# Moving operands on a 1152-byte pitch in a decoder trunk of float32 matmuls

## The chip, the cores and the metric

The kernel runs on one core of a Trainium2 chip. The metric is the device time of one execution in microseconds; a kernel is timed in several runs, and the median counts.

## The reference

A trunk of two layers over 528 tokens (16 learned meta tokens and 512 of the input) of width 1024. Each layer adds half a SwiGLU block, a mixer and half a second SwiGLU block to the residual stream, with an RMS norm ahead of each. The mixer of the first layer is chunked retention with four heads, that of the second is gated linear attention (GLA). All is float32.

```python
def swiglu(x, w_in, w_out):                  # w_in 1024 x 5632, w_out 2816 x 1024
    gate, up = jnp.split(x @ w_in, 2, axis=-1)
    return (jax.nn.silu(gate) * up) @ w_out

for i in range(2):
    h = h + 0.5 * swiglu(rmsnorm(h, norm_ffn1[i]), ffn1_w_in[i], ffn1_w_out[i])
    hn = rmsnorm(h, norm_mix[i])
    mix = retention(hn, ...) if i == 0 else gla(hn, ...)
    h = h + mix
    h = h + 0.5 * swiglu(rmsnorm(h, norm_ffn2[i]), ffn2_w_in[i], ffn2_w_out[i])
h = rmsnorm(h, final_norm)[:, 16:]
```

## The kernel before, in words

The residual stream lies transposed in SBUF: eight tiles x of 128 channels by 528 tokens. The stages follow each other: SwiGLU f10, retention, SwiGLU f20, SwiGLU f11, GLA, SwiGLU f21.

**A product in three.** Every float32 operand is split into a rounded high part and a low part, and a product is three matmuls in a row (mm3, lines 401 to 404): high weights with high tokens (L402), high weights with low tokens (L403), low weights with high tokens (L404). So the moving operands, the tokens, are read in the order high, low, high, then the same for the next block k of 128 input channels. Each matmul covers 264 tokens, half of the 528; in the last SwiGLU, f21, 256 tokens, since the meta tokens are no longer needed.

**Units.** Most projections are done as units: a 2 x 2 block product (two halves of the input channels, two output tiles, two halves of the tokens) in seven products instead of eight, by a Winograd form of Strassen's scheme. Its seven steps (unit_steps, from L589; the order is W.UNIT, L68) each take one weight matrix and one token matrix: a11 reads the first half of the tokens of the first four channel blocks (in uh and ul), a12 and s4 read the last four (both halves), and s1, s2, s3 and a22 read four sums of those, made once for each stage and kept in th (high) and tl (low). Each step is four blocks k and so twelve matmuls. For the output product of SwiGLU the hidden values of a pair of tiles are kept with their sums in tiles H, seven slots of high parts and seven of low ones.

**Where the moving operands lie.** The normed input: tiles uha and ula of 8 x 528 floats, so one block is 2112 bytes after another and the second half of the tokens 1056 after the first (L372 to L374). The sums: th and tl of 4 x 4 x 264 floats, block by block, the four sums of a block 1056 bytes apart (L666). H: 2 x 7 x 264 floats (L727). Retention's gated output og: 4 x 528 floats for each part. uh and ul are used again by every stage.

**Around the products.** Weights come by DMA on SP (raw) and with an accumulating DMA on POOL (pairs), are split by ScalarE (L160) and VectorE (L161) into whi and wlo, and are requested several products ahead. After each step of a unit, ScalarE or VectorE takes the result out of its PSUM bank; a unit has an evacuation tile su (four slots of 264 floats, three buffers, L636), and the values of a pair (gated, L703) and the sums that hidden makes of them (L728) use the same three buffers. u_sums (L573) makes the sums of the normed input of one block and splits all four at once; scaled (L473) writes one block of gained input as high part (ScalarE) and low part (VectorE) when the stage before hands it on; renorm (L694) writes the blocks again once the norm's factor is known. The framework sets the order of the work on each engine by the order of the program and by a head start given to evacuations (urgent, L379); an instruction waits for the tiles that it reads or overwrites.

Of the kernel before, what the change touches and what calls it, by code (L numbers as in the profile page):

```python
# [16 lines left out]
P = 128  # L17
# [35 lines left out]
PW = 512  # L53
AHEAD = 4
# [162 lines left out]

@with_exitstack
def trunk(ctx, tc, a):
# [135 lines left out]
    causal = const.tile([P, P], F32, name="causal")  # L355
    nc.sync.dma_start(causal, a["tri"][1])
    ctail = const.tile([3 * MR, MR], F32, name="ctail")
    for g in range(3):
        S.copy(ctail[g * MR:(g + 1) * MR], causal[g * MR:(g + 1) * MR, g * MR:(g + 1) * MR])
# [7 lines left out]
    half_neg = const.tile([P, 8], F32, name="half_neg")  # L367
    V.memset(half_neg, -0.5)
# [7 lines left out]
    rc = upool.tile([P, 8], F32, tag="rc", name="rc")  # L376

# [60 lines left out]
    def rsqrt_rows(sq, parts, width, name, finish):  # L438
# [13 lines left out]
        G.tensor_tensor(r[:w, :nj], ms[:w, :nj], half_neg[:w, :nj], ALU.pow)  # L452
# [12 lines left out]
    def enter(gcol, by, lag=1, lag2=1):  # L465
# [6 lines left out]

        def scaled(d, parts="hl"):  # L473
            g = gains[:, gcol + d:gcol + d + 1]
            hi, lo, src = uh[d][:, t0:], ul[d][:, t0:], x[d][:, t0:]
            with urgent():
                if "h" in parts:
                    S.activation(hi, src, AF.Copy, scale=g)
                if "l" in parts:
                    V.scalar_tensor_tensor(lo, src, g, hi.bitcast(F32), ALU.mult, ALU.subtract)  # L480
# [37 lines left out]
        def stats():  # L518
# [12 lines left out]
            for (b0, w, nb, m), c in zip(by, cols):  # L531
# [3 lines left out]
                G.tensor_tensor(r, ms[:w, :nb], half_neg[:w, :nb], ALU.pow)  # L535
# [28 lines left out]
    def t_sums(t, b22_b11, b12, b21):  # L564


        if b12 is not None:
            V.tensor_sub(t[:, :2], b22_b11, b12.unsqueeze(1).broadcast_to([P, 2, b12.shape[1]]))
            V.scalar_tensor_tensor(t[:, 2], b22_b11[:, 0], -1.0, t[:, 1], ALU.mult, ALU.subtract)
        if b21 is not None:  # L570
            V.scalar_tensor_tensor(t[:, 3], b21, -1.0, t[:, 2], ALU.mult, ALU.subtract)

    def u_sums(pool, name, halves, normed, hi, lo):  # L573
# [15 lines left out]
    def unit_steps(key, name, order, halves, nk, rhs, places, row1, c22, c21, behind=None):  # L589
# [8 lines left out]
        def step(q):  # L598
# [6 lines left out]
            for k in range(nk):  # L605
                with tc.issue_after(behind.ins) if behind else ExitStack():
                    ends["unit"] = mm3(to[into], *W.at(w, k * P), *rhs(what, k), k == 0 and into not in started,
                                       k == nk - 1, skip_group_check=True)
# [21 lines left out]
    def unit(key, name, order, halves, nk, rhs, pool, row1, c22, c21, behind=None):  # L630
# [8 lines left out]
        for st in unit_steps(key, name, order, halves, nk, rhs, places, row1, c22, c21, behind):  # L639
            st()  # L640

    def quarters(halves, th, tl):

        tl = tl if isinstance(tl, list) else [tl[:, k] for k in range(4)]
        wd = width(halves)

        def rhs(what, k):
# [4 lines left out]
            return th[:, k, i, :wd], tl[k][:, i, :wd]  # L652
# [4 lines left out]
    def ffn(which, layer, halves, gcol, feed, late=False):  # L657
# [5 lines left out]
        with tc.tile_pool(name=f"h_{me}", bufs=4) as hp, tc.tile_pool(name=f"t_{me}", bufs=1) as tp, \  # L663
                tc.tile_pool(name=f"u_{me}", bufs=3) as up_, psum_pool(4) as pp:
            other["pool"] = pp
            th, tl = [tp.tile([P, 4, 4, 264], F32R, tag=f"t{i}", name=f"t{i}{me}") for i in "hl"]  # L666
            rhs_in = quarters(halves, th, tl)
            H, normed = {}, {}
            groups = GROUPS if feed else LAST_GROUPS

            def place(j):


                if j not in normed:
                    t = hp.tile([P, 4 * T + 4 * 264], F32, tag="H", name=f"un{me}{j}")
# [12 lines left out]
            def sums(j):  # L688
                norm(j)
                for i in range(2):  # L690
                    k = 2 * j + i
                    u_sums(up_, f"{me}{k}", halves, normed[j][:, i].rearrange("p h t -> p (h t)"), th[:, k], tl[:, k])

            def renorm():  # L694
                for h, r0, r1 in ((0, a0, a1), (1, a0, a1), (1, b0, b1)):
                    for j in range(2):
                        k = 4 * h + 2 * j
                        split(uha[:, k:k + 2, r0:r1], ula[:, k:k + 2, r0:r1], normed[j][:, :, 1 - h, r0:r1])
# [4 lines left out]
            def gated(f):  # L703
# [4 lines left out]
                return up_.tile([P, 4, 264], F32, tag="su", name=f"y{me}{f}")[:, :, :wd]  # L708

            def hidden(f, y, part=None):  # L710

                gi = [g[0] <= f < g[1] for g in groups].index(True)
                if feed is None and gi == len(groups) - 1:
                    h = hp.tile([P, 2, 2, T], F32R, tag="H", name=f"h{me}{f}")
                    for i in range(2):
                        split(pair(h[:, 0, i, :], halves), pair(h[:, 1, i, :], halves), y[:, 2 - 2 * i:4 - 2 * i])
                elif part == 1:
                    h, t = halfway.pop()
# [1363 lines left out]
```

## Time and profile before

| | |
|---|---|
| median of three runs | 2070.16 us (2069.03 to 2070.55) |
| the profiled execution's own time | 2071.41 us |
| its span | 2069.6 us |
| TensorE busy | 2057.5 us, 16335 matmuls |
| weight loads busy | 2012.9 us |
| VectorE busy | 1790.8 us |
| ScalarE busy | 1200.2 us |
| GpSimd busy | 208.8 us |

A matmul's duration in the profile (about 285 ns for 264 columns) holds its way through the array and overlaps the next ones; how fast they follow each other is read from their start times. A group's line names the line of the kernel, the engine, the operation, output and inputs with buffer numbers left out, the shape and the count, then busy time in us, mean ns of one, and the idle time ahead of it.

### The profile page before, as it was taken

To read this page: it belongs to the slowest core of one execution; us is meant where nothing else is said; L and a number is where in the kernel's file an instruction comes from. 1 tells how busy PE (TensorE), PEld (TensorE's weight loads), DVE (VectorE), ACT (ScalarE), POOL (GpSimd) and SP (SyncE) were. 2 spreads that over 40 slices of the span, in tenths; PEclk is the share of its full clock that TensorE was granted. 3 is DMA by queue.
4 is the path that set the end of the run, shared out by engine and by line. 5 is a ranking of instruction groups with operands and counts; after the bars stand their busy time and mean duration, and the time that the engine had idled before them with its cause. 6 is when DMAs were issued, how large, how long until landed. Compare 5 with 4: busy or idle time off the path is not lost.

```text
span 2069.6 us, 42946 instructions
## 1 busy us (share of the span) xinstructions
PE 2057.5 (99%) x16335; PEld 2012.9 (97%) x16335; DVE 1790.8 (87%) x3218; ACT 1200.2 (58%) x2365; POOL 208.8 (10%) x181
## 2 busy tenths in 40 slices
PE   9999999999999999999999999999999999999998
PEld 9999999999999999999999999999999988999998
DVE  8988889978686889988889998889897968998886
ACT  5756566554545455656666565666645445666664
POOL 1011111010101000111111011111001000111110
PEclk9999999999999999999999999999999999999999
DMA  7676777355555532776776476677614351687772
GB/s 224 154 193 158 193 185 185 107 144 132 146 132 138 136 104 70 184 191 158 195 188 172 111 180 179 162 197 177 194 57 119 91 165 61 161 214 174 183 179 72
DMA packets 176112, 318.84 MB, mean 154 GB/s; under 512 B 17569, under 2 KB 40737, under 8 KB 175905
## 3 DMA queue, kind: packets, MB, share of 16 engines
q1 hardware_dynamic: 133856, 237.04, 34.6%
q0 software_dynamic: 40896, 75.51, 23.5%
q10 hardware_dynamic: 1152, 3.55, 0.5%
q8 instruction: 128, 2.10, 0.4%
q14 instruction: 80, 0.65, 0.1%
HBM read 311.76 MB, written 4.26 MB: 153 GB/s over the span
## 4 chain that ended last, share of the span: by engine, by line
PE 95%; DVE 2%; ACT 1%; issue 1%; DMA 0%; POOL 0%; SPq 0%; POOLq 0%; ACTq 0%; DVEq 0%
PE po_r L403 2%; PE po_r L402 2%; PE po_r L404 2%; PE Xf20o L402 1%; PE Xf10o L402 1%; PE Xf11o L402 1%; PE Xf10o L404 1%; PE Xf10o L403 1%; PE Xf20o L403 1%; PE Xf20o L404 1%; PE Xf11o L403 1%; PE Xf11o L404 1%; PE lv L1614 1%; PE Xf20u L402 1%; PE Xf11u L402 1%; PE Xf21u L404 1%
## 5 line engine op out<-in xcount | busy, mean ns | idle before, releaser
L160 ACT CAST whi<-raw 128x512 fp32r<-128x512 f32 (+1 forms) x893 | 525.6, 606 | 482.3 <-DVE raw L166 92.2
L161 DVE TENSOR_TENSOR wlo<-raw,whi 128x512 fp32r<-128x512 f32 (+1 forms) x893 | 584.1, 669 | 143.8 <-ACT whi L160 134.7
L160 ACT CAST whi<-pair 128x512 fp32r<-128x512 f32 (+1 forms) x304 | 183.5, 604 | 122.2 <-PE Xf11u L403 7.3
L161 DVE TENSOR_TENSOR wlo<-pair,whi 128x512 fp32r<-128x512 f32 (+1 forms) x304 | 202.0, 664 | 6.4 <-ACT whi L160 5.0
L129 POOL DMA_DIRECT2D pair<-in_f_in x73 | 88.5, 1213 | 725.4 <-DVE wlo L161 313.6
L166 DVE TENSOR_TENSOR raw<-pair,raw 128x512 f32<-128x512 f32 (+1 forms) x146 | 97.3, 667 | 2.6
L168 DVE TENSOR_TENSOR raw<-raw,raw 128x512 f32<-128x512 f32 (+1 forms) x146 | 97.3, 666 | 2.5
L129 POOL DMA_DIRECT2D pair<-in_f_out x44 | 53.2, 1208 | 379.1 <-DVE wlo L161 208.8
L402 PE MATMUL po_r<-ogh,whi 128*128 128x264 f32 x256 | 73.0, 285 | 0.0
L403 PE MATMUL po_r<-ogl,whi 128*128 128x264 f32 x256 | 73.0, 285 | 0.0
L404 PE MATMUL po_r<-ogh,wlo 128*128 128x264 f32 x256 | 72.8, 285 | 0.0
L129 POOL DMA_DIRECT2D pair<-in_ret_in x20 | 24.3, 1215 | 301.8 <-DVE wlo L161 90.7
L402 PE MATMUL Xf20o<-hf,whi 128*128 128x264 f32 x176 | 50.8, 289 | 0.2
L402 PE MATMUL Xf11o<-hf,whi 128*128 128x264 f32 x176 | 50.8, 289 | 0.2
L402 PE MATMUL Xf10o<-hf,whi 128*128 128x264 f32 x176 | 50.8, 289 | 0.2
L403 PE MATMUL Xf10o<-hf,whi 128*128 128x264 f32 x176 | 50.0, 284 | 0.0
L403 PE MATMUL Xf11o<-hf,whi 128*128 128x264 f32 x176 | 50.0, 284 | 0.0
L403 PE MATMUL Xf20o<-hf,whi 128*128 128x264 f32 x176 | 50.0, 284 | 0.0
L404 PE MATMUL Xf10o<-hf,wlo 128*128 128x264 f32 x176 | 49.9, 284 | 0.0
L404 PE MATMUL Xf11o<-hf,wlo 128*128 128x264 f32 x176 | 49.9, 284 | 0.0
L404 PE MATMUL Xf20o<-hf,wlo 128*128 128x264 f32 x176 | 49.9, 284 | 0.0
L402 PEld LDWEIGHTS po_r<-ogh,whi 128*128 128x128 f32 x256 | 48.3, 189 | 0.0
(1007 smaller groups left out, 8523.8 us busy)
## 6 DMA issues: line engine op xcount, KB each, us to landing
raw<-in_f_in SPq DMA_DIRECT2D x277, 256.0 KB, 4.5
pair<-in_f_in SPq DMA_DIRECT2D x150, 256.0 KB, 4.7
pair<-in_f_in POOLq DMA_DIRECT2D x73, 512.0 KB, 6.7
raw<-in_f_out SPq DMA_DIRECT2D x80, 256.0 KB, 3.7
raw<-in_ret_in SPq DMA_DIRECT2D x76, 256.0 KB, 3.3
raw<-in_f_out SPq DMA_DIRECT2D x72, 192.0 KB, 3.2
pair<-in_f_out SPq DMA_DIRECT2D x48, 256.0 KB, 3.9
pair<-in_f_out POOLq DMA_DIRECT2D x24, 512.0 KB, 6.1
```

Of the source, the lines that this page charges most:

```text
L129: nc.gpsimd.dma_start(t, aps[2].unsqueeze(1).broadcast_to([P, 2, n]), accum_op=ALU.add)
L160: self.nc.scalar.copy(hi[:, :n], raw)
L161: V.tensor_sub(lo[:, :n], raw, hi[:, :n].bitcast(F32))
L166: V.tensor_add(s2, self.tiles[c][:, 1], self.tiles[c, "a11"])
L168: V.tensor_add(raw, raw, s2)
L402: nc.tensor.matmul(ps, lhsT=lh, rhs=rh, start=start, stop=False, **kw)
L403: nc.tensor.matmul(ps, lhsT=lh, rhs=rl, start=False, stop=False, **kw)
L404: return nc.tensor.matmul(ps, lhsT=ll, rhs=rh, start=False, stop=stop, **kw)
L1614: nc.tensor.matmul(ps[:, j, J * P:J * P + n], lhsT=Kt[:, j, J * P:(J + 1) * P], rhs=q, start=(J == 0), stop=(J == 3), skip_group_check=True)
```

## The change

The tiles of moving operands get another layout. A slot of 264 tokens is laid 1152 bytes (288 floats, HP_) after the one before instead of 1056. The tile of low parts is placed, by an empty block of 128 bytes ahead of it, at 128 bytes mod 256 from the tile of high parts. Further empty blocks (SKEW_W, SKEW_S, SKEW_R) stand ahead of the tiles of evacuation and weights.

- The normed input of f10, retention, f20 and f11 (class Split) has twelve slots in the u tiles and four in new n tiles: the first half of the tokens of blocks 0 to 3, both halves of blocks 4 to 7 in slots 4 to 11, and the second half of blocks 0 to 3 in n. That part is needed only ahead of the units; then the two n tiles serve as evacuation tiles, in turn. Blocks 0 to 3 are therefore scaled in two instructions for each part.
- For GLA and f21 (class Whole) a block keeps its tokens in one row, at a pitch of 544 and 512 floats.
- th and tl are laid slot by slot, the four blocks of a sum 1152 bytes apart. In f21 the pitch is 256 floats and there is no offset.
- H has fourteen slots of that pitch, so that the low part's seven start 128 mod 256 after the high part's, and 128 bytes at the end of a tile shift the next one against it; in the group with four pairs the odd slots are read in the order 1, 0, 3, 2.
- The sums are made in two halves in two buffers of their own (t_pair), so u_sums and hidden split them in two instructions for each part instead of one.
- Retention's triangular mask is loaded at the beginning of retention; its copy for the last rows is gone, and that product is done in strips of 32 rows. Retention no longer writes the second half of blocks 0 to 3 again.
- The constant of the power on GpSimd lies in a column of rc, and the room for DMA descriptors of GpSimd is halved.

The core of the diff:

```diff
-    uha = upool.tile([P, KD, T], F32R, tag="uh", name="uha")
-    ula = upool.tile([P, KD, T], F32R, tag="ul", name="ula")
-    uh, ul = [[t[:, d, :] for d in range(KD)] for t in (uha, ula)]
+    def u_tiles(name):
+        ts = []
+        for i in "hl":
+            ts.append([upool.tile([P, n * KD // 2 * HP_], F32R, tag=t + i, name=f"{t}{i}{name}") for t, n in (("u", 3), ("n", 1))])
+            if i == "h":
+                skew(upool, 4 * FLIP, f"uskew{name}")
+        return ts
+    class Split:
+        def begin(self):
+            self.t, c = zip(*[[t.rearrange("p (d c) -> p d c", c=HP_)[:, :, :HT] for t in ts] for ts in u_tiles(self.name)])
+            self.rows = [[Halves(None, [t[:, d], n[:, d]]) for d in range(KD // 2)] +
+                         [Halves(t[:, d::KD // 2]) for d in range(KD // 2, KD)] for t, n in zip(self.t, c)]
+        def views(self, d, t0, src):
+            rows = [r[d] for r in self.rows]
+            if d >= KD // 2:
+                return [(*[r.both for r in rows], pair(src, HALVES))]
+            return [(*[r.each[h] for r in rows], src[:, h * HT:(h + 1) * HT]) for h in range(2)]
...
-            hi, lo, src = uh[d][:, t0:], ul[d][:, t0:], x[d][:, t0:]
-            with urgent():
-                if "h" in parts:
-                    S.activation(hi, src, AF.Copy, scale=g)
-                if "l" in parts:
-                    V.scalar_tensor_tensor(lo, src, g, hi.bitcast(F32), ALU.mult, ALU.subtract)
+            for hi, lo, src in u.views(d, t0, x[d]):
+                with urgent():
+                    if "h" in parts:
+                        S.activation(hi, src, AF.Copy, scale=g)
+                    if "l" in parts:
+                        V.scalar_tensor_tensor(lo, src, g, hi.bitcast(F32), ALU.mult, ALU.subtract)
...
-        t = pool.tile([P, 4, 264], F32, tag="su", name=f"tt{name}")[:, :, :wd]
         t_sums(t, mid, normed[:, T + b0:T + b1], normed[:, a0:a1])
-        split(hi[:, :, :wd], lo[:, :, :wd], t)
+        for i in range(2):
+            split(hi[:, 2 * i:2 * i + 2], lo[:, 2 * i:2 * i + 2], t[i])
...
-            su = pool.tile([P, 4, 264], F32, tag="su", name=f"su{name}")[:, :, :wd]
+            su = place()
...
+    def spare():
+        return in_turn([lambda i=i: upool.tile([P, 4, HP_], F32, tag="n" + i, name=f"su{count[0]}")[:, :, :HT] for i in "hl"])
...
-            th, tl = [tp.tile([P, 4, 4, 264], F32R, tag=f"t{i}", name=f"t{i}{me}") for i in "hl"]
+            th = tp.tile([P, 4, 4, pitch], F32R, tag="th", name=f"th{me}")
+            skew(tp, 4 * flip, f"skew{me}t")
+            tl = tp.tile([P, 4, 4, pitch], F32R, tag="tl", name=f"tl{me}")
...
-                    h = hp.tile([P, 2, 7, 264], F32R, tag="H", name=f"h{me}{f}")
-                    t = up_.tile([P, 4, 264], F32, tag="su", name=f"tt{me}h{f}")[:, :, :wd]
+                    h = h_tile(f"h{me}{f}")
+                    hi, lo = h = [h[:, o:o + 7 * pitch].rearrange("p (q t) -> p q t", q=7)[:, :, :wd]
+                                  for o in (0, 7 * pitch)]
+                    t = t_pair(tmp, ("hf", "hf"), f"{me}h{f}", wd)
...
                         split(hi[:, :3], lo[:, :3], y[:, :3])
-                        split(hi[:, 3:], lo[:, 3:], t)
+                        for i in range(2):
+                            split(hi[:, 3 + 2 * i:5 + 2 * i], lo[:, 3 + 2 * i:5 + 2 * i], t[i])
...
+                def ks(what):
+                    return ODD if flip and len(hs) == 4 and slot(what) % 2 else range(len(hs))
...
-    nc = bacc.Bacc("TRN2", target_bir_lowering=False, num_devices=1, dynamic_dma_scratch_size=2048)
+    nc = bacc.Bacc("TRN2", target_bir_lowering=False, num_devices=1, dynamic_dma_scratch_size=1024)
```

More of the change, by code (lines that the diff above doesn't have):

```diff
@@ L53 @@
 PW = 512
+HT = T // 2
+HP_ = 288
+FLIP = 32
+ODD, BACK = (1, 0, 3, 2), 48
+SKEW_W, SKEW_S, SKEW_R = 160, 192, 64
 AHEAD = 4
@@ L215, in less, with __init__, __getitem__ @@
         self.ahead = AHEAD
+class Halves:
+    def __init__(self, both, each=None):
+        self.both, self.each = both, each or [both[:, h] for h in range(2)]
+    def __getitem__(self, at):
+        r0, r1 = at[1].start, at[1].stop
+        if r1 - r0 == T:
+            return self.both
+        h = r0 // HT
+        return self.each[h][:, r0 - h * HT:r1 - h * HT]
 @with_exitstack
@@ L604, in step @@
             w = W.get(key + (q,))
-            for k in range(nk):
+            turn = ks(what)
+            for k in turn:
                 with tc.issue_after(behind.ins) if behind else ExitStack():
-                    ends["unit"] = mm3(to[into], *W.at(w, k * P), *rhs(what, k), k == 0 and into not in started,
-                                       k == nk - 1, skip_group_check=True)
+                    ends["unit"] = mm3(to[into], *W.at(w, k * P), *rhs(what, k), k == turn[0] and into not in started,
+                                       k == turn[-1], skip_group_check=True)
             started.add(into)
@@ L628, in unit_steps, with rows4, unit @@
         return [lambda q=q: step(q) for q in order]
-    def unit(key, name, order, halves, nk, rhs, pool, row1, c22, c21, behind=None):
+    def rows4(what):
+        return range(4)
+    def unit(key, name, order, halves, ks, rhs, place, row1, c22, c21, behind=None):
         wd = width(halves)
@@ L888, in c21 @@
                         feed(d + 1, ins)
-                unit((which, layer, "o", gi, d), f"{me}o{gi}{d}", W.UNIT, halves, len(hs), rhs, up_, row1, c22, c21, behind)
+                unit((which, layer, "o", gi, d), f"{me}o{gi}{d}", W.UNIT, halves, ks, rhs, place_of[0], row1, c22, c21, behind)
             first, outs, g = True, {}, []
@@ L1416, in gla @@
             th = gp.tile([P, 4, 4, 264], F32R, tag="th", name="gth")
+            th = [th[:, k] for k in range(4)]
+            uh, ul = u.rows
             tl, normed = [], []
@@ L1986, in gla @@
             out_proj("g1", lambda dp: ("go", 1, dp), hh, hl, (TOKENS,), 1.0, feed, per=2)
-    feed = enter(G_F1, BY_P, 4)
+    u1, ur, u2, u3 = [Split(n) for n in ("f10", "ret", "f20", "f11")]
+    ug, u4 = Whole("gla", T + 16, (0, 0)), Whole("f21", 2 * P * 2, (BACK, BACK - FLIP))
+    feed = enter(G_F1, BY_P, u1, 4)
     W.fetch(2)
```

226 lines of the change are left out of this document (141 added, 85 removed).

## The prediction

> **What bounds the kernel now.** I read the page's busy times first, then the chain of waits, then the list of who waits for whom, then the instructions in order of time. The page and its chain:
>
> ```profile
> span 2069.6 us, 42946 instructions
> PE 2057.5 (99%) x16335; PEld 2012.9 (97%) x16335; DVE 1790.8 (87%) x3218; ACT 1200.2 (58%) x2365; POOL 208.8 (10%) x181
> ...
> PE 95%; DVE 2%; ACT 1%; issue 1%; DMA 0%; POOL 0%; SPq 0%; POOLq 0%; ACTq 0%; DVEq 0%
> ```
>
> TensorE is busy for 99% of the span and holds 95% of the chain, so the other engines matter only where they make it wait. The waits of TensorE, longest in total first (what waited, for whom, us, times, longest):
>
> ```profile
> PE idle L366 <- DVE half_neg L368: 1.1, 1, 1.1
> PE st_n L524 <- DVE sqa_n L495: 0.9, 1, 0.9
> PE sc L402 <- ACT krh L1254: 0.5, 2, 0.3
> ```
>
> They come to a few microseconds. So the time is the number of matmuls times the distance from one start to the next, and that distance must be read from start times: the duration of one (0.28 us) overlaps its neighbours. The three stretches that hold only SwiGLU work (columns: stretch, length, then busy time and count of PE, PEld, DVE, ACT, POOL, then granted clock, DMA share, GB/s):
>
> ```profile
> 850.00:950.00 100.00, 100.00 (x823) 99.95 (x822) 87.93 (x147) 59.29 (x115) 12.11 (x10) 1.00 0.72 180
> 950.00:1060.00 110.00, 110.00 (x901) 109.71 (x900) 96.79 (x171) 69.25 (x138) 14.53 (x12) 1.00 0.72 182
> 1800.00:2030.00 230.00, 230.00 (x1930) 228.70 (x1929) 205.85 (x377) 142.58 (x296) 29.93 (x26) 1.00 0.73 184
> ```
>
> 100 us over 823 matmuls is 121.5 ns for 264 columns, 110 over 901 is 122.1, and 230 over 1930 is 119.2 for 256 columns. The clock is granted in full (1.00), so the throttle is not what stretches them.
>
> Does the distance depend on the addresses that the change moves? One whole unit of seven products, twelve matmuls each, in the third SwiGLU group of the second stage, by its instructions in order of time (start us, duration):
>
> ```profile
> 1042.48 0.28 PE L402 MATMUL Xf20g<-uha,whi 128*128 128x264 f32 x1
> ...
> 1043.94 0.29 PE L402 MATMUL QZf20g<-thf,whi 128*128 128x264 f32 x1
> ...
> 1045.40 0.28 PE L402 MATMUL Xf20g<-thf,whi 128*128 128x264 f32 x1
> ...
> 1046.86 0.28 PE L402 MATMUL QZf20g<-uha,whi 128*128 128x264 f32 x1
> ...
> 1048.33 0.28 PE L402 MATMUL Xf20g<-thf,whi 128*128 128x264 f32 x1
> ...
> 1049.79 0.28 PE L402 MATMUL QZf20g<-uha,whi 128*128 128x264 f32 x1
> ...
> 1051.23 0.29 PE L402 MATMUL Xf20g<-thf,whi 128*128 128x264 f32 x1
> ...
> 1052.71 0.28 PE L402 MATMUL Xf20u<-uha,whi 128*128 128x264 f32 x1
> ```
>
> The steps take 1.46, 1.46, 1.46, 1.47, 1.46, 1.44 and 1.48 us, the unit 10.23 us, or 121.8 ns a matmul. In the memory layout of the program uha starts at byte 21472 of each partition and thf at 182528; a row is 264 x 4 = 1056 bytes. So the moving operands of steps 3, 5 and 6 start at multiples of 64 bytes, those of 1, 2, 4 and 7 at 32 past one. The aligned three take 4.36 us for 36, 121.1 ns; the others 5.87 us for 48, 122.3 ns. High and low part lie 0 mod 256 apart in all seven. So the address has an effect, of about 1% between these sets.
>
> One place already does half of what the change does: retention's output product reads ogh (byte 168192) and ogl (199552), 128 mod 256 apart, rows 64 further by each k. Two steps of twelve there:
>
> ```profile
> 570.83 0.28 PE L402 MATMUL po_r<-ogh,whi 128*128 128x264 f32 x1
> ...
> 572.30 0.28 PE L402 MATMUL po_r<-ogh,whi 128*128 128x264 f32 x1
> ...
> 573.77 0.29 PE L402 MATMUL po_r<-ogh,whi 128*128 128x264 f32 x1
> ```
>
> 1.47 us each, 122.5 ns, though the first starts at multiples of 64. Two of three neighbours there alternate by 128, and it is no faster than the average.
>
> **The change, part by part.** (1) *Pitch and offset.* Every moving operand of f10, f20, f11 and retention starts at a multiple of 128 (1152 = 9 x 128, if the added blocks put the tiles' bases on one), and each is 128 mod 256 from the one before. The number of matmuls: per SwiGLU stage 9 pairs x 2 units x 84 = 1512 inner, 11 hidden pairs x 7 x 3 x 4 = 924 outer, 384 plain in the first (in the others 288 plain and one unit of 84 more): 2820 + 2 x 2808. Retention: 192 for q and k and 192 for v of the first head, 6 + 6 + 8 units of 84, and 768 out: 2832. In all 11,268; at 0.1218 us they are two thirds of the span. No row shows operands that alternate throughout. Bounds from the rows: the best of one kind is the sixth step's 1.44 us, 120.0 ns, so -1.8 ns x 11,268 = -20 us; the worst the seventh's 1.48 us, 123.3 ns, +1.5 ns, +17 us. Below the first lies what a start with no stall would give: the shortest distances stand singly, as 0.11 us here, and rounding leaves 100 to 120 ns:
>
> ```profile
> 1044.19 0.28 PE L404 MATMUL QZf20g<-thf,wlo 128*128 128x264 f32 x1
> 1044.30 0.28 PE L402 MATMUL QZf20g<-thf,whi 128*128 128x264 f32 x1
> ```
>
> At 115 throughout it would be -6.8 ns, -77 us. I take the aligned steps' 121.1 ns: -0.7 ns x 11,268 = -7.9 us, because alignment is what these rows show to matter, and the one place that alternates shows nothing more.
>
> By the Trainium skill (SBUF — State Buffer, "Who interferes with whom") TensorE has two read ports of its own, one for the moving operand and one for the weights, and never waits on anyone; TensorE: Matmul & The Clock Gate, "Back-to-back issue gap", gives a distance from the column count and the clock alone, which for 264 would be 112.5 ns (estimate from that page). By these the addresses are indifferent and part 1 is worth nothing; the trace has 121.8 ns, and 1.44 against 1.48 us for steps that differ in addresses and not in size, so it does not fit them fully.
>
> (2) *The last stage* (f21, 256 columns, pitch 1024, no offset): there alignment moves from 1056 to 1024, with no alternation. About 2,350 matmuls of 119.2 ns; between -1.8 and +1.5 ns as above, -4 to +4 us; I take 0, since no row here tells the two apart.
>
> (3) *Split instructions.* u_sums and hidden now write their four sums in two halves, and four of eight rows are scaled by halves. The rows, from 25 to 470 us (count, busy us, mean ns):
>
> ```profile
> L436 DVE TENSOR_TENSOR tlf<-ttf,thf 128x1056 fp32r<-128x1056 f32 x4 | 4.9, 1251 | 0.0
> L436 DVE TENSOR_TENSOR ula<-unf,uha 128x528 fp32r<-128x528 f32 x6 | 4.0, 700 | 0.0
> L480 DVE SCALAR_TENSOR_TENSOR ula<-x,gains,uha 128x528 fp32r<-128x528 f32 x8 | 6.1, 761 | 0.0
> L569 DVE SCALAR_TENSOR_TENSOR ttf<-unf,ttf 128x264 f32<-128x264 f32 x4 | 1.5, 426 | 0.0
> L435 ACT CAST thf<-ttf 128x1056 fp32r<-128x1056 f32 x4 | 4.1, 1076 | 2.5 <-DVE ttf L571 2.5
> L435 ACT CAST uha<-unf 128x528 fp32r<-128x528 f32 x6 | 3.4, 628 | 0.0
> ```
>
> A split of 1056 into two costs VectorE 2 x 700 - 1251 = 149 ns and ScalarE 2 x 628 - 1076 = 180 ns; 20 in u_sums and about 39 in hidden make 8.8 and 10.6 us. A scaling by halves costs VectorE 2 x 426 - 761 = 91 ns, 16 of them 1.5 us. VectorE idles for 2069.6 - 1790.8 = 279 us, ScalarE for more, and TensorE's queue of products covers it. The cover is thinnest where each stage begins:
>
> ```profile
> 25.00:100.00 75.00, 75.00 (x611) 74.43 (x610) 72.67 (x123) 44.84 (x81) 6.05 (x5) 1.00 0.58 150
> ```
>
> VectorE has 2.3 us left of 75 there. Six more halves (four u_sums, two hidden) are 0.9 us; if that cover were gone at each of four beginnings, 3.6 us. I take +1.
>
> (4) *Buffers.* The evacuation tiles fall from three to two, and the sums of hidden move to a shared pair. The next unit's first ScalarE copy out of the bank then waits for hidden to have read its values: about five sums and splits of 0.4 to 1.3 us, some 5 us, against a unit of 10.23 us. Hidden by that unit: 0. Were it exposed, each of some 40 pairs could lose a microsecond.
>
> (5) *Small things.* The mask moves from the start to retention (one DMA on SP behind weight loads that are requested several products ahead), three small ScalarE copies leave the start, the mask's multiply becomes three, two renormalisations of retention go (-2.7 us of cover), POOL's power reads another constant, and POOL's descriptor room is halved while its queue is 10% busy. All lie beside TensorE's work: 0, at most 1 us either way.
>
> Sum: -7.9 + 0 + 1 = -6.9 us. The profiled execution took 2071.41 us, 1.8 more than its span, and 1.25 more than the median 2070.16 of the runs; from it 2064.5, by the median 2063.3. I say **2063**; its own range, with the rest of parts 2 to 5, is 2057 to 2069.
>
> **The rivals.** *The alternation takes away the stall itself.* For it: 121.8 ns against single distances of 0.11 us, a regular excess that no semaphore explains, and steps whose times differ by address. Against it: po_r alternates in two of three starts and has 122.5. If the distance falls halfway to 112, to 117 ns, it is -4.8 ns x 11,268 = -54 us: 2016 by the median. *The alternation is the bad pattern* (the other side). In po_r the aligned step alone costs 1.47 us where aligned steps without alternation cost 1.44 to 1.46; if 122.5 ns becomes the rule everywhere, +0.7 x 11,268 = +7.9 us and +1 for part 3: 2079; it decides as soon as the alternated distance is above 121.8. With the seventh step's 123.3 it would be 2088. *Addresses don't matter here*: the step times differ for another reason (which product, which bank), the layout is neutral, and parts 3 to 5 remain, 2070 to 2073. This is what the two pages of the Trainium skill would say.
>
> **How the numbers follow.** The forecast (alignment counts, alternation adds nothing) gets 0.40, the stall's removal 0.25, the bad pattern 0.22, no effect 0.13. A measurement of this kernel can tell about 0.2%, 4.1 us, from no change: under 2066.0 is faster, over 2074.3 slower. Of the forecast's 0.40, 0.30 falls below 2066; with the second case 0.55 faster. 0.10 of the forecast and 0.12 of no effect are the same, 0.22; the bad pattern and a last hundredth are slower, 0.23. The range has to reach into both other cases: 2015 to 2081 leaves out the lower half of the stall's removal and the worst of the bad pattern, together about 0.2.
>
> **What would show it.** Step 1 is right if twelve matmuls of an inner unit take 1.45 us in every step of the unit, the aligned and the formerly misaligned alike; 1.40 or less would be the first rival, 1.47 or more in all steps the second, the old mixture of 1.44 to 1.48 the third. Part 3 shows as more VectorE time (about 1800 us) with TensorE's waits as short as now; part 4 is wrong if ScalarE's copies out of the banks (L614 to L620 now) wait for VectorE and TensorE's list of waits names them. The prediction falls if the three stretches above change by more than 2% a matmul, or if TensorE's idle time grows past 20 us.

## The result, and the profile after

| | before | after |
|---|---|---|
| median of the runs, on the same chip | 2070.48 us (2069.03 to 2074.36, 6 runs) | 2059.24 us (2057.91 to 2060.26, 6 runs) |
| the profiled execution's own time | 2071.41 us | 2058.71 us |
| TensorE busy, of the span | 2057.5 of 2069.6 us | 2030.9 of 2056.9 us |
| TensorE not busy | 12.1 us | 26.0 us |

The ratio of the times is 0.9944, with a 95% interval of 0.9931 to 0.9957: the changed kernel is 0.56% faster. The time lies 4 us under the forecast of 2063, but it did not come about in the way that the forecast described. The page of the changed kernel, the lines that answer to those shown of before:

```profile
span 2056.9 us, 43086 instructions
PE 2030.9 (99%) x16335; PEld 1973.7 (96%) x16335; DVE 1795.5 (87%) x3299; ACT 1199.0 (58%) x2435; POOL 210.4 (10%) x181
...
PE 36%; DVE 6%; ACT 1%; issue 1%; DMA 1%; POOL 0%; POOLq 0%; SPq 0%; DVEq 0%; ACTq 0%
```

TensorE has lost 26.6 us of busy time with the same 16335 matmuls. The chain on this page is followed back from the end to 1122 us only, so that its shares add up to 45% and not to 99% as before. TensorE holds 36 of these 45, VectorE 6; before it was 95 of 99 and 2. So the chain now passes through VectorE more often. The same four stretches (columns as before: stretch, length, busy time and count of PE, PEld, DVE, ACT, POOL, then granted clock, DMA share, GB/s):

```profile
25.00:100.00 75.00, 70.97 (x577) 69.50 (x577) 69.63 (x121) 44.10 (x83) 4.88 (x4) 0.98 0.55 140
850.00:950.00 100.00, 99.35 (x829) 98.54 (x828) 88.35 (x153) 60.07 (x120) 13.26 (x11) 1.00 0.74 183
950.00:1060.00 110.00, 109.77 (x913) 108.20 (x912) 98.34 (x178) 67.96 (x142) 13.53 (x12) 1.00 0.74 184
1800.00:2030.00 230.00, 229.94 (x1952) 227.09 (x1952) 205.74 (x379) 142.58 (x300) 28.33 (x24) 1.00 0.71 176
```

The three SwiGLU stretches hold 0.7%, 1.3% and 1.1% more matmuls than before (waits are in these figures), and the start holds fewer (577 against 611), at a granted clock of 0.98. What happens inside a unit is seen from start times. The unit that the prediction showed, the third SwiGLU group of f20, now (start us, duration):

```profile
1036.33 0.28 PE L473 MATMUL Xf20g<-uhf,whi 128*128 128x264 f32 x1
...
1037.73 0.28 PE L473 MATMUL QZf20g<-thf,whi 128*128 128x264 f32 x1
...
1039.13 0.28 PE L473 MATMUL Xf20g<-thf,whi 128*128 128x264 f32 x1
...
1043.33 0.28 PE L473 MATMUL QZf20g<-uhf,whi 128*128 128x264 f32 x1
...
1044.62 0.28 PE L475 MATMUL QZf20g<-uhf,wlo 128*128 128x264 f32 x1
1044.82 0.39 PE L473 MATMUL Xf20g<-thf,whi 128*128 128x264 f32 x1
1045.04 0.29 PE L474 MATMUL Xf20g<-tlf,whi 128*128 128x264 f32 x1
1045.17 0.29 PE L475 MATMUL Xf20g<-thf,wlo 128*128 128x264 f32 x1
1045.29 0.29 PE L473 MATMUL Xf20g<-thf,whi 128*128 128x264 f32 x1
...
1046.37 0.28 PE L473 MATMUL Xf20u<-uhf,whi 128*128 128x264 f32 x1
```

The first five steps take exactly 1.40 us each (1036.33 to 1043.33), where the first five took 1.46 or 1.47 before. That is 116.67 ns a matmul, the same in every step, whatever it reads. The sixth step ends late: the next matmul starts 0.20 us after the one before it instead of 0.12, the one after that 0.22 later, and the whole seventh step takes 1.55 us at 0.12 to 0.13 us a matmul. What made it late was VectorE:

```profile
1043.72 0.69 DVE L168 TENSOR_TENSOR wlo<-raw,whi 128x512 fp32r<-128x512 f32 x1
1044.33 0.43 DVE L942 TENSOR_TENSOR gf<-Xf20g,su 128x264 f32<-128x264 f32 x1
```

L942 is the sum for c22, one of the unit's four output blocks; it reads the bank X, to which the seventh step adds. It stood behind a weight split and ended at 1044.76; the matmul started at 1044.82. So the unit takes 10.04 us instead of 10.23: a gain of 0.43 us by pace, 0.24 of it lost again by one wait of less than 0.1 us and what follows it.

For a reading of all stages I took the distances from one start to the next from the traces, and parted them. The *pace* of a stage is the mean of those up to 140 ns for its matmuls of 264 columns (137 for 256). A *wait*, counted over all matmuls of 256 columns and more, is a distance over 162 ns for 264 columns, and its excess is what goes beyond 122 ns; for other widths both limits shift by 1 ns for every 2.4 columns. One wait of the engine can give two such distances, as 0.20 and 0.22 us above, and the matmuls at half speed that are shown below count too.

| | before | after |
|---|---|---|
| pace of f10, f20, f11 (264 columns) | 121.8, 121.8, 121.8 ns | 118.0, 117.9, 117.8 ns |
| pace of retention (264) | 121.9 ns | 118.9 ns |
| pace of f21 (256) | 118.2 ns | 115.6 ns |
| waits (long distances), their excess | 283, 39.0 us | 475, 71.3 us |

With the counts of the prediction the pace is worth 3.8 x 2820 + 3.9 x 2808 + 4.0 x 2808 + 3.0 x 2832 + 2.6 x 2352 = 47.5 us. The waits took 32.3 of it. The difference, 15.2, stands to 12.7 measured in the two profiled executions; the excess is counted from 122 ns in both kernels, so some 2 us of the new waits lie in neither number.

The waits of TensorE, longest first (what waited, for whom, us, times, longest):

```profile
PE pf10g L475 <- DVE wlo L168: 3.9, 2, 3.7
PE sc L473 <- DVE vl L630: 1.4, 1, 1.4
PE idle L382 <- DVE rc L444: 1.1, 1, 1.1
PE sc L473 <- DVE pl L507: 1.0, 4, 0.4
PE pf10g L473 <- ACT whi L167: 0.8, 1, 0.8
PE st_n L599 <- DVE sqa_n L572: 0.8, 1, 0.8
```

The first is at the start of f10, and more follows from it:

```profile
50.46 0.39 PE L475 MATMUL pf10g<-uhf,wlo 128*128 128x264 f32 x1 [3.69 <-DVE wlo L168]
50.69 0.28 PE L473 MATMUL pf10g<-uhf,whi 128*128 128x264 f32 x1
...
51.82 0.42 PE L473 MATMUL pf10g<-uhf,whi 128*128 128x264 f32 x1
52.04 0.42 PE L474 MATMUL pf10g<-ulf,whi 128*128 128x264 f32 x1
...
54.90 0.39 PE L475 MATMUL pf10g<-nhf,wlo 128*128 128x264 f32 x1
55.12 0.29 PE L473 MATMUL pf10g<-nhf,whi 128*128 128x264 f32 x1
```

After the wait TensorE runs at its pace for 1.3 us, and then 15 matmuls follow at 0.22 us each, from 51.82 to 55.12: half speed for 3.3 us, 1.5 us lost. A second such stretch, of 14, begins near 21 us, behind the wait of st_n. The trace of before has neither. The windows of the profile show the clock (columns as above):

```profile
48.29:51.70 3.41, 1.24 (x10) 1.24 (x11) 3.41 (x8) 1.39 (x2) 0.00 (x0) 1.00 0.06 13
51.70:55.11 3.41, 3.41 (x17) 3.41 (x17) 3.41 (x6) 0.00 (x0) 0.00 (x0) 0.50 0.85 275
```

By the Trainium skill (TensorE: Matmul & The Clock Gate, "What's actually happening") the clock is halved after an idle window of about 3.4 us, and the windows run on by themselves and don't begin with the idleness. The length agrees: the granted clock is 0.50 for 3.41 us. That the window ahead has to be idle does not: in the 3.41 us ahead TensorE was busy for 1.24 us here, and for 2.65 us ahead of the stretch near 21 us. What decides it stays open.

### The profile page after: what moved, and what is told of

It reads as the page before. It is cut to its first block, busy times and chain, and to the rows that moved or that the text cites. A ratio compares the mean times of both kernels' runs of the same rounds, so it can differ in the third digit from the quotient of the medians.

```text
span 2056.9 us, 43086 instructions
## 1 busy us (share of the span) xinstructions
PE 2030.9 (99%) x16335; PEld 1973.7 (96%) x16335; DVE 1795.5 (87%) x3299; ACT 1199.0 (58%) x2435; POOL 210.4 (10%) x181
## 3 DMA queue, kind: packets, MB, share of 16 engines
q10 hardware_dynamic: 1152, 3.55, 0.5%
## 5 line engine op out<-in xcount | busy, mean ns | idle before, releaser
L167 ACT CAST whi<-pair 128x512 fp32r<-128x512 f32 (+1 forms) x304 | 183.9, 605 | 95.4 <-ACT su L695 12.7
```

The costliest lines, as they stand in the source:

```text
L167: self.nc.scalar.copy(hi[:, :n], raw)
```

## The experiments

Two questions were open: what sets the pace, and where the new waits come from. The ratios are against the kernel before, run on the same chip; a difference to the changed kernel is one of medians from different chips, on which the kernel before took 2070.2 to 2071.3 us.

**Alternation or alignment: e1_noflip.** All starts stay multiples of 64 at a pitch of 1152, but the low parts come to lie 0 mod 256 from the high ones. The addresses of GLA and f21 are kept.

```diff
-            if i == "h":
-                skew(upool, 4 * FLIP, f"uskew{name}")
+        skew(upool, 4 * FLIP, f"uskew{name}")      # behind the low part; th, tl and rtl likewise
...
-                                  for o in (0, 7 * pitch)]
+                                  for o in (0, 7 * pitch + flip)]
```

> The changed kernel with the 128 bytes behind the low part instead of in front of it (u, the t sums, the hidden tiles), so that low and high part start at the same address mod 256; pitch, 64-byte alignment, split instructions and buffers stay. Theory A (the forecast: only the 64-byte alignment counts, alternation adds nothing): distances stay at 117.9 ns and the time at 2059 us, within 3. Theory B (first rival: the alternation itself takes a stall away): two of three successions lie in the same 128-byte half again, the 264-column matmuls of the first three SwiGLUs and the retention (some 9,200) go back to 121 to 122 ns, +35 us. The new waits tell two more apart. B1, they come from the second evacuation buffer that was given up and the split instructions: they stay at about 75 us in all and the time is 2088 to 2095. B2, they come because TensorE is faster than VectorE's work allows: they fall back to about 40 us and the time is 2064 to 2074.

Measured: 2069.45 us, ratio 0.9995 (0.9986 to 1.0003). One unit by its start times:

```profile
1042.97 0.28 PE L472 MATMUL Xf20g<-uhf,whi 128*128 128x264 f32 x1
...
1044.42 0.28 PE L472 MATMUL QZf20g<-thf,whi 128*128 128x264 f32 x1
...
1045.88 0.28 PE L472 MATMUL Xf20g<-thf,whi 128*128 128x264 f32 x1
...
1053.14 0.28 PE L472 MATMUL Xf20u<-uhf,whi 128*128 128x264 f32 x1
```

The unit takes 10.17 us, 121.1 ns a matmul, and the pace of f10, f20 and f11 is 121.3 ns. So theory A is out and theory B holds: of the 3.9 ns, all that this kernel keeps (the multiples of 64, the pitch, the place of the weights) brings 0.5 (121.8 to 121.3), and the offset of the low parts 3.4. The waits fell to 53.0 us, between the two rivals' numbers; those at the start stayed, those ahead of s2 and a22 in the inner units (up to two for one such wait) went from 102 to 27. So B2 explains the larger part of these.

**Are all successions needed: e2_order.** In the changed kernel 475 successions of matmuls still start in the same 128-byte half: in the outer units of each first group, whose four tiles were filled in the order 0, 2, 1, 3; between retention's uh (64 mod 256) and its sums rth (192 mod 256); and from one half of retention's output to the next. The edit changes the order of k, and no address.

```diff
+                    if flip and len(hs) == 4 and gi == 0:
+                        return ((0, 2, 1, 3), (2, 0, 3, 1))[slot(what) % 2]
...
+    def rows_r(what):                              # retention's units
+        return ODD if what in ("n3", "t1", "t2", "t4") else range(4)
...
-                for k in range(k0, k1):
+                turn = [k ^ 1 for k in range(k0, k1)] if swap and hf else range(k0, k1)
+                for k in turn:
```

> The changed kernel with three orders of k turned round, no address changed: in the outer units of the first group (0,2,1,3) or (2,0,3,1), in the retention's sums (1,0,3,2), in the second half of the retention's output (1,0,3,2), so that successive moving operands alternate by 128 mod 256 there too (475 successions in the same half become 112). Theory A: nothing but noise, 2059. Theory B: the first group's outer steps go from 119.6 to 122.4 ns a matmul to 116.7 (1,008 matmuls, -3.7 us), the retention's inner steps from 120.8 and 117.5 to 116.7 (-4.4 us), its output from 119.2 to 116.7 (-1.9 us): 2049 if no wait grows, up to 2054 if the waits take half of it.

Measured: 2050.25 us, ratio 0.9907 (0.9893 to 0.9920), 9.0 us less than the changed kernel, as theory B has it. A unit of retention in the changed kernel, and behind it the same unit here:

```profile
522.73 0.28 PE L473 MATMUL QZrg<-uhret,whi 128*128 128x264 f32 x1
...
524.18 0.28 PE L473 MATMUL Xrg<-rth,whi 128*128 128x264 f32 x1
...
525.59 0.28 PE L473 MATMUL QZrg<-uhret,whi 128*128 128x264 f32 x1
```

```profile
519.39 0.28 PE L473 MATMUL QZrg<-uhret,whi 128*128 128x264 f32 x1
...
520.79 0.28 PE L473 MATMUL Xrg<-rth,whi 128*128 128x264 f32 x1
...
522.19 0.28 PE L473 MATMUL QZrg<-uhret,whi 128*128 128x264 f32 x1
```

1.45 and 1.41 us became 1.40 and 1.40, and retention's pace went from 118.9 to 117.3 ns. A step whose own twelve reads alternate throughout still took 1.45 us, only because its first read lay in the same half as the last read before it. So a disturbance is carried on: nine matmuls at 120 to 125 ns after the change from rth to uh, two after the change back.

**The weights' place: e8_w64 and e11_w0.** The moving operands start at 64 or 192 mod 256 and the weight tiles at 128. In e8_w64 the weights lie 64 bytes lower, at 64; in e11_w0 128 lower, at 0.

```diff
-SKEW_W, SKEW_S, SKEW_R = 160, 192, 64
+SKEW_W, SKEW_S, SKEW_R = 96, 256, 128              # e11_w0: 32, 320, 192
...
-            skew(wp, SKEW_R, "mskew")
+            skew(wp, SKEW_R - 128, "mskew")
```

> The changed kernel with all weight tiles 64 bytes lower (64 mod 256 in place of 128), moving operands of the SwiGLUs and the retention where they were. If the place of the weights against the moving operands takes part in the pace: the steps of the first three SwiGLUs leave 116.67 ns, anywhere up to 122, 2060 to 2100. If only the succession of the moving operands counts: 2057 to 2061.

> The changed kernel with the weight tiles 128 bytes lower (0 mod 256 in place of 128; the retention's two extra tiles stay), moving operands where they were (64 and 192 mod 256). e8_w64 showed that weights at 64 mod 256 cost the lock. If what counts is that weights and moving operands lie 64 apart mod 128: 116.67 ns stays, 2057 to 2062. If weights have a place of their own in the alternation mod 256: 118 to 122 ns, 2062 to 2095.

Measured: e8_w64 2082.42 us, ratio 1.0058 (1.0045 to 1.0070); e11_w0 2061.30 us, ratio 0.9949 (0.9935 to 0.9962). In e8_w64:

```profile
1046.03 0.29 PE L473 MATMUL Xf20g<-uhf,whi 128*128 128x264 f32 x1
...
1047.49 0.29 PE L473 MATMUL QZf20g<-thf,whi 128*128 128x264 f32 x1
...
1056.25 0.29 PE L473 MATMUL Xf20u<-uhf,whi 128*128 128x264 f32 x1
```

Every step takes 1.46 us, 121.7 ns a matmul, although all moving operands of the unit alternate. In e11_w0 f10, f20 and f11 keep 117.7 to 117.9 ns, and a step takes 1.40 us:

```profile
1035.94 0.28 PE L473 MATMUL Xf20g<-uhf,whi 128*128 128x264 f32 x1
...
1037.34 0.28 PE L473 MATMUL QZf20g<-thf,whi 128*128 128x264 f32 x1
```

So, of the layouts tried, the pace needs both: moving operands that alternate, and weights that lie 64 mod 128 away from them. f21 bears this out: its moving operands lie at 64, like the weights of e8_w64, and its pace there is 119.9 ns, the slowest of all kernels. In both edits raw weights and temporaries of other engines shift with the weight tiles; the split weights, which TensorE reads, were not moved alone. e8_w64 answers the question of the waits too. It has the changed kernel's split instructions, buffers and orders at the old pace, and its waits come to 42.8 us, against 39.0 before: 3.8 us are the price of the rearranged work itself, and the other 28 us came with the pace (the two stretches at half speed, some 3 us, among them).

**256 columns: e7_f21alt.** In f21 all moving operands lie at 64 mod 256. Here the low parts get the offset there too, so that two of three successions alternate.

```diff
-    ... Whole("f21", 2 * P * 2, (BACK, BACK - FLIP))
+    ... Whole("f21", 2 * P * 2, (BACK, BACK))
...
-        pitch, flip = (HP_, FLIP) if feed else (wd, 0)
+        pitch, flip = HP_ if feed else wd, FLIP
...
-                                  for o in (0, 7 * pitch)]
+                                  for o in (0, 7 * pitch + (0 if feed else flip))]
```

> The changed kernel with the low parts 128 bytes off the high ones in the last SwiGLU too (256 columns of 1,024 bytes at a pitch of 1,024 or 2,048; 2,352 matmuls at 115.6 ns, which lay all at the same address mod 256): two of three successions alternate there now. If alternation is what every matmul wants: nearer 113.3 ns, -4 to -6 us, 2053 to 2055. If it is only wanted where a row isn't a whole number of 256-byte blocks (264 columns, 1,056 bytes), equal addresses were right for 256 columns, which e1_noflip ran at 113.3 ns in part: no gain or a loss, 118 to 121 ns, 2059 to 2072.

Measured: 2061.30 us, ratio 0.9963 (0.9950 to 0.9975); f21's pace went from 115.6 to 117.7 ns. The second alternative holds, at its mild end (its pace was to be 118 to 121). 115.6 is a mean over two paces, each of which keeps up by itself: in the changed kernel's f21 one step and, later, another with the same addresses mod 256:

```profile
1775.26 0.28 PE L473 MATMUL Xf21g<-uhf,whi 128*128 128x256 f32 x1
...
1776.62 0.28 PE L473 MATMUL QZf21g<-thf,whi 128*128 128x256 f32 x1
...
1848.77 0.28 PE L473 MATMUL Xf21g<-thf,whi 128*128 128x256 f32 x1
...
1850.19 0.28 PE L473 MATMUL QZf21g<-uhf,whi 128*128 128x256 f32 x1
```

1.36 us and 1.42 us for twelve, which is 113.3 ns and, by the mean of the stretch around the second, 117.8. f21 goes from one to the other only at a disturbance, a wait or a few distances of 119 to 125 ns, in either direction. How that decides it stays open; it moved f21 by up to 4 us between kernels that leave its addresses alone (115.5 ns in e9_order_early, 117.3 in e10_mild).

**The wait at the start: e3_early.** The splits of five weight blocks of f10 are put ahead of the second block of sums in VectorE's order.

```diff
+                if 12 <= i < 17:
+                    order_.enter_context(self.tc.high_priority(offset=HEAD_START))
                 self.nc.scalar.copy(hi[:, :n], raw)
                 V.tensor_sub(lo[:, :n], raw, hi[:, :n].bitcast(F32))
```

> The changed kernel with the split of five weight blocks of the first SwiGLU put ahead of the second block of sums in VectorE's order. If the wait of pf10g for wlo at 50 us (3.85 us, and the 15 matmuls behind it at half rate, 1.5 us) comes from that order alone: both go, 2054. If VectorE is simply full there: the wait goes to the sums or to the next weights and the time stays at 2058 to 2060.

Measured: 2055.41 us, ratio 0.9928 (0.9915 to 0.9940), 3.8 us less than the changed kernel. The start again:

```profile
25.00:100.00 75.00, 72.50 (x607) 71.36 (x606) 72.43 (x128) 45.43 (x87) 6.19 (x6) 1.00 0.59 148
```

607 matmuls instead of 577, at the full clock. The order was the cause there, and it came with the change: in the trace of before two of these splits ran between the sums, at 43.93 us, and in the changed kernel they came behind them, at 49.72.

**A third evacuation buffer: e4_third.** The tile of the squares and one more of 2112 bytes serve as a third buffer; the room is that of one of seven raw weight buffers.

```diff
-    def __init__(self, tc, ctx, raw_bufs=7, pair_bufs=3, bufs=7):
+    def __init__(self, tc, ctx, raw_bufs=6, pair_bufs=3, bufs=7):
...
+        n = [...]                                   # the two n tiles
...
+        return n[1] if y else in_turn([mine, n[0]]) # y: gated values; else su
```

> The changed kernel with a third buffer for the SwiGLU's sums (the squares' tile and one more of 2,112 bytes; one raw weight buffer of seven is given up for it), all addresses of moving operands and weights the same mod 256. B1 (the new waits come from two buffers): the waits ahead of s2 in the inner units (42, 7.2 us) nearly go, with the loss of pace behind them (some 50 ns each): 2049 to 2053. B2 (TensorE is too fast for VectorE): they stay to within 2 us, 2057 to 2061.

Measured: 2069.57 us, ratio 0.9994 (0.9985 to 1.0003), 10.3 us more than the changed kernel. The waits ahead of s2 in the inner units stayed at 42, of 7.2 us, and those ahead of a22 went from 60 to 57: B1 is out. The loss lies elsewhere, mostly in retention (excess 4.4 to 10.5 us), which doesn't use the third buffer. Two stretches at half the clock, 6.8 us from 415.2 us and 3.4 us from 469.8, are part of that. The missing weight buffer is the likely cause, but that was not tried alone.

**Snapshots ahead of weights: e5_snap, e6_all, e10_mild.** Why are s2 and a22 late? One s2 in the changed kernel, ScalarE's work:

```profile
1279.76 1.65 ACT L167 CAST whi<-raw 128x512 fp32r<-128x512 f32 x3
1281.32 0.38 ACT L695 COPY su<-Xf11u 128x264 f32<-128x264 f32 x1
```

The copy of X, which s2 overwrites, stood behind three casts and ended at 1281.70. TensorE's last matmul ahead of s2 had started at 1281.39, and s2 began at 1281.74, 0.35 us later instead of 0.12. e5_snap puts the copy after a11 and the first sum of c22 ahead of the weight splits issued there, and splits no weights after a22. e6_all adds e2_order and e3_early.

```diff
+                if q == "a11":
+                    copied = S.copy(ab[:, int(first)], X)
+                elif q == "s3":
+                    summed = c22(X, s_[:, 0])
+            hook(q != "a22", (copied, summed))
-            hook()
...
+                with self.tc.issue_after(self.after[0].ins) if self.after[0] else ExitStack():
                     self.nc.scalar.copy(hi[:, :n], raw)
```

In these two kernels the sum put ahead in retention changes the values that retention computes; kind and number of the engines' operations are the same.

> The changed kernel with the snapshots of the bank X put ahead of the weight splits: after a11 ScalarE's copy of X comes before the casts issued at that point, after s3 VectorE's first sum of c22 comes before the subtractions issued there, and after a22 no weights are split. Theory W1: the new waits ahead of s2 and a22 come from that order (at 1279.8 us ScalarE did three casts of 0.57 us ahead of a copy that TensorE waited for), with steps of 1.40 us in place of 1.46. Then the 42 waits of the inner units ahead of s2 (7.2 us) and the 60 ahead of a22 (7.7 us) fall to less than a quarter, and with the pace lost behind each the time is 2042 to 2048. Theory W2: VectorE is full there, and weights or sums come late in place of the snapshots: 2055 to 2062, with waits for wlo.

> The three orders of k of e2_order, the early weights of e3_early and the snapshots of e5_snap in one kernel. The first two alone gave -9.0 and -3.8 us, which should add up, since they lie in different stages: 2046.4. By W1 the snapshots take another 11 to 17: 2030 to 2036. By W2 they take nothing: 2045 to 2049.

Measured: e5_snap 2107.96 us, ratio 1.0185 (1.0171 to 1.0199); e6_all 2103.24 us, ratio 1.0155 (1.0141 to 1.0169). New among the waits of e5_snap:

```profile
PE QZf10g L482 <- DVE wlo L170: 3.6, 8, 0.5
PE QZf11g L482 <- DVE wlo L170: 3.6, 8, 0.5
PE QZf20g L482 <- DVE wlo L170: 3.6, 8, 0.5
```

The waits ahead of s2 went from 42 to 14, and 67 ahead of a12 (22 us) and 84 ahead of s3 (13 us) came: the weights are late now. Those ahead of a22 stayed at 7 us. The kind of wait is W2's; the times lie some 50 us above the ranges of both theories. One gap in the splits of every unit is not made good here.

e10_mild keeps splitting after every step, leaves retention's sums where they were, and stands on e2_order and e3_early together, which is e9_order_early.

> The three orders of k of e2_order and the early weights of e3_early, without the snapshots. Alone they gave -9.0 and -3.8 us; they lie in different stages, so if both causes are right they add up: 2046.4, within 2. If the early weights only moved a wait that a faster stage behind them meets again: 2049 to 2051.

> As e9_order_early, with the milder half of e5_snap: ScalarE's copy of X after a11 ahead of the casts issued at that point, and in the SwiGLUs VectorE's first sum of c22 ahead of the subtractions issued there; weights are split after every step again. If e5_snap was slow only because no weights were split after a22 (its waits ahead of a12 and s3, 35 us): the waits ahead of s2 and a22 fall without new ones, 2032 to 2042. If ScalarE's and VectorE's order has no place to give (each snapshot moved ahead makes weights late): 2047 to 2065, with waits ahead of a12 or s3 in place of s2.

Measured: e9_order_early 2050.38 us, ratio 0.9895 (0.9880 to 0.9909); e10_mild 2047.30 us, ratio 0.9878 (0.9865 to 0.9892), the fastest kernel of the study. In e10_mild the waits ahead of a22 in the inner units went from some 60 to 2 (8 to 0.8 us), in the outer ones from some 50 to 9, and those ahead of s2 from some 40 to 30. So the order was at fault for a22, W1 there, but the gain expected with it did not come: longer waits stand at other places, st_n for 2.4 us and tv for 1.7, and f21 ran at 117.3 ns instead of 115.5, which is 4.2 us. The intervals of the two kernels overlap, so that e10_mild beats e9_order_early is not shown. Nor is it settled that the two gains in e9_order_early add up. Its four runs spread with the granted clock: 2053.43 us at 0.996, 2051.31 at 0.997, 2049.46 at 0.998, 2045.08 at 1.000. The last one is near the sum, 2046.4. In the profiled execution, the slowest, the granted clock was 0.50 for 6.8 us from 409.6 us and for 6.8 us from 1116.1; e3_early has the first of these stretches too, and neither of the two kernels has the second.

## Why the prediction was right, and where it was wrong

The number was right by luck; the mechanism of its largest term was not.

*What bounds the kernel.* Right: time is the number of matmuls times their distance, and 47.5 us of pace came from nothing else.

*Part 1, alignment counts and "alternation adds nothing": wrong.* Taken: -0.7 ns. Measured: -0.5 ns with alignment but without the offset (e1_noflip), and another -3.4 by the offset. Nor do the operands start at multiples of 128, as part 1 assumed: they start at 64 and 192 mod 256, and by e8_w64 just this place against the weights counts. The term of -7.9 us was -41.4 in the four stages. The step that failed is the reading of po_r as a place that "already does half of what the change does". It had two of three successions alternating and weights at 0 mod 256, while its rows moved by 64 from k to k, so that in the first half of the tokens every other k started 0 mod 128 from the weights. e2_order shows that one succession in the same half can hold up to nine matmuls at the slow pace, and e8_w64 that weights 0 mod 128 away cost all of it; so a place with one bad succession in three, and a quarter of its starts so placed, shows nothing of a place with neither. The bound of 120.0 ns from the best step was too narrow for the same reason.

*Part 2, f21 at 0, between -4 and +4 us: wrong, a little outside.* 118.2 became 115.6 ns, 6.1 us. It moves between 113.3 and 117.8 ns at each disturbance, and no run shows what decides.

*Part 3, split instructions at +1, up to 3.6: nearly right at the old pace.* e8_w64 gives 3.8 us, and they lie where the cover was said to be thinnest, at the start. VectorE got 4.7 us more work; forecast were 8.8 + 1.5, less 2.7 of renormalisations that go.

*Part 4, buffers at 0: right as far as shown.* A third buffer, with one weight buffer less, took hardly a wait away (60 to 57 ahead of a22), and at the old pace two buffers have no more waits ahead of s2 than three had (none in e8_w64, 7 before).

*Part 5:* nothing of it shows.

*The cover.* What no step had is that the waits depend on the pace. VectorE's 279 us of idle time and the queue of products were taken as cover; but a snapshot of X has one step's time to pass two engines' queues, and from 1.46 to 1.40 us that was no longer enough: there are 192 more long distances. That the order on the two engines is at fault is shown for a22 (e10_mild) and argued for the rest. The pace brought 28 us of waits against its own 47.5.

*The rivals.* The first, the stall's removal, is what happened, with 0.25. Its price of -4.8 ns was near (-3.9 in the three SwiGLUs), its time of 2016 was not, since it let TensorE keep all of it. The bad pattern did not occur as such; its evidence, po_r's 122.5 ns, had the bad succession and the bad place against the weights, and the runs don't part the two there. That addresses don't matter is refuted by e1_noflip and e8_w64. By the Trainium skill (SBUF — State Buffer, "Who interferes with whom") TensorE never waits on anyone. These two kernels differ from the changed one in addresses only and lose 3.4 and 3.9 ns a matmul, so the measurement decides that addresses are not indifferent; whether TensorE then waits on another engine or on its own reads, no run shows.

*What would show it.* 1.40 us a step was named as the sign of the first rival, and that is what the trace shows. Idle time past 20 us was named as what makes the prediction fall; it is 26.0. The other sign, a change of more than 2% a matmul in the three stretches, stayed away (at most 1.3%), since they hold the new waits with the pace. So the number of 2063 came out near 2059 by luck: two errors, 39.6 us of pace (47.5 against 7.9) and 31.3 us of waits (32.3 against 1), nearly cancelled.

## What to carry to other kernels

Where a matmul reads at a distance that its column count and the clock don't explain, look at the start addresses of successive operands and of the weights, and judge a layout only by a stretch in which every succession follows it: one exception in twelve can cost most of the gain. A faster bounding engine turns slack into waits: ahead of a forecast, take the shortest time that another engine has to answer in, and not its idle total. And a wait may cost more than itself: here half speed for 3.3 us behind waits of 0.8 and 3.7 us, and the loss of the pace behind those of 0.1.

## What the runs showed of the hardware

- In the changed layout and undisturbed, the pace of 264 columns is one value, 116.67 ns. For 256 it is one of two, 113.33 or 117.8. In the layouts without it the distances of 264 columns scatter, in the kernel before mostly from 116 to 127 ns about 121.8. With the 2.4 GHz that the Trainium skill gives (TensorE: Matmul & The Clock Gate, "What's actually happening") 116.67 and 113.33 are 280 and 272 cycles, the columns and 16 more. The same page ("Back-to-back issue gap") has columns / 2.4 + 2.5 for a matmul by itself, 112.5 ns for 264 as an estimate; no stretch here reached it.
- Of the layouts tried for rows of 1056 bytes, only that with starts alternating by 128 mod 256 and weights 64 mod 128 away from them has the fast pace (117.8 ns in the mean of a stage; 121.3 without the first, 121.7 without the second). Rows of 1024 bytes that all start alike, with the same place of the weights, have both of their paces and change only at a disturbance. Why the addresses count, no run shows.
- A disturbance lasts: after a repeated half or a wait of under 0.1 us, mostly two to eleven matmuls follow at 119 to 129 ns.
- A thousandth of the granted clock is 2 us of this kernel. The clock goes along with the spread of e9_order_early's runs (2045.08 us at 1.000, 2053.43 at 0.996), but doesn't explain that of e10_mild's (2042.38 us at 0.997, 2046.88 at 0.997).
